# Seven half-depth products for the branch and last projections of a hybrid mLSTM and attention block

## The chip, the cores and the metric

The kernel is one program on one core of a Trainium2 chip. The metric is the device time of one execution in microseconds (us), here the median of several runs on the same chip. Engines are called as the profile calls them: PE is TensorE's matrix products, PEld its loads of the stationary operand, DVE is VectorE, ACT is ScalarE, POOL is GpSimd, and SP is the queue that issues most DMAs. A line such as L291 is a line of the kernel before.

## The reference

One layer on x of 1024 x 1024 in float32: a norm, one wide projection by w_in, an mLSTM branch in two directions, a branch of differential attention, and then the part that the change concerns, the tail:

```python
y_a = hm * jax.nn.sigmoid(a_o) * jax.nn.silu(a_z)
...
y_b = att.reshape(B, S, DA_WIDTH).astype(x.dtype) * jax.nn.silu(b_z)
gb = gate_b[layer]
mix = (jax.nn.sigmoid(g_a + gb[0]) * jnp.einsum('bsc,cd->bsd', y_a, w_branch_a[layer])
       + jax.nn.sigmoid(g_b + gb[1]) * jnp.einsum('bsc,cd->bsd', y_b, w_branch_b[layer]))
x = x + jnp.einsum('bsd,de->bse', mix, w_out[layer])
return rmsnorm(x, final_g)
```

Each of the three products is 1024 x 1024 by 1024 x 1024.

## The kernel before

Every operand of a float32 product is split into a high half H (the value rounded to the type that TensorE multiplies) and a low half L (what the rounding left), and a product is the three terms H·H, H·L and L·H. So an output block of 128 x 512 over a depth of 1024, which is 8 blocks of 128, takes 24 matmuls. A split is a copy on ACT for H and a subtraction on VectorE or POOL for L.

The program is a list of units, most of them a few matmuls with what follows them, in an order written out by hand in `build` (from L1463 on) and partly interleaved by `Weaver`. `run` goes through the list. TensorE keeps the order of the list. The instructions of the other engines and of SP are put in order by a scheduler that takes what is ready, earlier units first; on the chip each engine then goes through its own list in order. A tile of a pool has a tag and a number of buffers; a new tile of the tag waits until the instructions that use the old one are done.

**The stage that has seven products already.** The projections of the mLSTM branch (L1472 to L1542) take their output columns in 16 pairs of blocks of 128. A pair with both halves of the sequence (512 columns of the moving operand each) is four output blocks of 128 x 512, that is a 2 x 2 product of 2 x 2 blocks with a depth of 512 each. `pair_units` (L270) makes it in seven products (f = 0 to 6) of sums and differences of the blocks, 12 matmuls each, in place of eight. `load_form` (L230) makes the stationary form of product f: forms 0, 4 and 6 are blocks as they are, 1, 2, 3 and 5 are sums, made by POOL (L243, L254); then ACT rounds H (L262) and VectorE (f = 0, 4, 6) or POOL makes L (L264). A form takes half a weight slot; `run` loads forms up to four keys past the next one, six half slots in all. The moving forms (`hH`, `hL`, `TH`, `TL`) are made once in the opening. Products 0, 1, 2 and 6 add up in one PSUM bank X, with ACT copies of it taken after 0, 1 and 2 (L298); 3 and 5 in a bank G, 4 in a bank F. A sink gets the finished blocks. In the order of the list (L1538), product 0 of a pair is followed by 6 of the pair before, 3, 5 of the pair before, 1, 4, 2.

**The tail.** After the mLSTM part the last three of sixteen gate projections run (`gate_units`, three groups of 48 matmuls), the last of them woven with loads of yb by `load_y` (L1310): a DMA of 128 x 1024 into one of two raw buffers, a copy on ACT (L1314), a subtraction on VectorE (L1315). Then `mix_units` for branch b and for branch a: for each of 8 blocks of output columns and each half of the sequence, 24 matmuls through `proj` (L429); the weights of the next block come through one DMA, one ACT copy (L204) and one POOL subtraction (L209). Its `done` multiplies by the gate (L1339), or adds the second branch to the mix and splits it (L1341 to L1345). The operands ya and the rows of w_out (`load_wo`, L1369 and L1370) are loaded and split in the course of the passes. `out_units` makes the last projection in 8 blocks of rows x 2 halves, 24 matmuls each (L1399); the last half of the last block is cut in two of 256 columns. Then come the residual (L1403), the sum of squares on ACT (L1405), the norm (`rsqrt`, with its power on POOL, L147), and the stores (L1418, L1420).

Of the kernel before, what the change touches and what calls it, by code (L numbers as in the profile page):

```python
# [109 lines left out]
class Block:  # L110
    def __init__(self, tc, A):
        self.tc, self.nc, self.A = tc, tc.nc, A
        nc = self.nc
        self.v, self.a, self.p, self.t, self.q = nc.vector, nc.scalar, nc.gpsimd, nc.tensor, nc.sync
        self.wt = {}
        self.raws = {}
        self.ml, self.opening, self.ahead, self.terms, self.forms = False, True, False, {}, 0
        self.rs, self.tk, self.loaded = {}, {}, set()
# [58 lines left out]
    def load_w(self, key, nxt=None):  # L177
# [3 lines left out]
        if key[0] == "sw":  # L181
            return self.load_form(key)
# [29 lines left out]
        if nxt and self.ahead:  # L212
            self.load_raw(("w_in", OFF["bq"] + nxt[1] * 128) if nxt[0] == "rope" else nxt)
# [5 lines left out]
    def pair_raws(self, p):  # L219
        if p >= len(self.pairs) or p in self.praws:  # L220
            return
        self.praws[p] = raws = []
        for seg, i in self.pairs[p]:
            pool = self.wpool if p % 2 == 0 else self.s0
            t = pool.tile([128, 8, 128], F32, name="raw", tag="raw", **({} if p % 2 == 0 else dict(bufs=2)))
            o = OFF[seg] + 128 * i
            self.q.dma_start(out=t, in_=self.A["w_in"][0][:, o:o + 128].rearrange("(k p) e -> p k e", p=128))
            raws.append(t)

    def load_form(self, key):  # L230
        _, p, f = key
        a, g = self.a, self.p
        self.pair_raws(p)
        if p == 0:
            self.pair_raws(1)
        r1, r2 = self.praws[p]
# [4 lines left out]
        lo, hi = slice(0, 4), slice(4, 8)  # L241
        tmp = lambda n: self.s0.tile([128, 4, 128], F32, name=n, tag=n, bufs=1)
        sub = lambda out, x, y: g.tensor_tensor(out=out, in0=x, in1=y, op=ALU.subtract)  # L243
        if f == 0:
            src = r1[:, lo]
        elif f == 1:
            self.s2f = src = tmp("s2f")
            sub(src, self.s1f, r1[:, lo])
        elif f == 2:
            src = tmp("s3f")  # L250
            sub(src, r1[:, lo], r2[:, lo])
        elif f == 3:
            self.s1f = src = tmp("s1f")
            g.tensor_tensor(out=src, in0=r2[:, lo], in1=r2[:, hi], op=ALU.add)  # L254
        elif f == 4:
            src = r1[:, hi]
        elif f == 5:
            src = self.s2f
            sub(src, r1[:, hi], src)
        else:  # L260
            src = r2[:, hi]
# [4 lines left out]
        if f == 5:  # L266
            del self.praws[p]
            self.pair_raws(p + 2)

    def pair_units(self, p, sink):  # L270
# [3 lines left out]
        v, a = self.v, self.a  # L274
        B = lambda half, o: (self.hH[half][:, o:o + 4], self.hL[half][:, o:o + 4])
        T = lambda i: (self.TH[i], self.TL[i])

        plan = lambda: (B(0, 0), T(1), T(2), T(0), B(0, 4), B(1, 4), T(3))
        box = {}
        u = lambda n, bufs=1: self.s0.tile([128, 512], F32, name=n, tag=n, bufs=bufs)  # L280

        def product(f, k0):
            bH, bL = plan()[f]
# [4 lines left out]
            wH, wL = self.wt[("sw", p, f)]  # L288
# [19 lines left out]
        return [[Unit(6 * MM, lambda f=f, k0=k0: product(f, k0), (("sw", p, f),)) for k0 in (0, 2)] for f in range(7)]  # L308
# [77 lines left out]
    def run(self, units):  # L386
# [10 lines left out]
        for i, u in enumerate(units):  # L397
            if u.keys:
                need = max(order.index(k) for k in u.keys) + 1

                room = lambda k: sum(1 if x[0] == "sw" else 2 for x in self.wt) + (1 if k[0] == "sw" else 2) <= 6
                ahead = lambda k: nxt < need or nxt <= need + (4 if k[0] == "sw" else 1) and room(k)
                while nxt < len(order) and (order[nxt] in self.loaded or not self.opening
                                            and (order[nxt][0] != "sw" or hasattr(self, "_s0")) and ahead(order[nxt])):
# [905 lines left out]
    def load_y(self, src, i, slot):  # L1310
        raw = self.wy.tile([128, S], F32, name="yraw", tag="yraw", bufs=2)
        self.q.dma_start(out=raw, in_=src[i])
        h, l = slot("H"), slot("L")
        self.a.copy(h, raw)  # L1314
        self.v.tensor_tensor(out=l, in0=raw, in1=h.bitcast(F32), op=ALU.subtract)  # L1315
        return h, l

    def slot(self, which, dt=F32R):
        pool, bufs = {"yb": (self.wy, 16), "mb": (self.wy, 8), "r": (self.wr, 16)}[which]
        return pool.tile([128, S], dt, name="sl_" + which, tag=which, bufs=bufs)  # L1320

    def mix_units(self, seg, st):
        v, a, p, q = self.v, self.a, self.p, self.q

        def start(i):
            t = self.wy.tile([128, S], F32, name="tgl", tag="tgl", bufs=2)
            q.dma_start(out=t, in_=self.tg[seg][i])
            st["tg"] = t
            if seg == "gb":
                st["m", i] = self.slot("mb", F32)  # L1330
            else:
                w = "r" if i < 4 else "mb" if i < 7 else "yb"
                st["mix", i] = (self.slot(w), self.slot(w))

        def done(i, half, ps):
            c = slice(half * 512, (half + 1) * 512)
            t, m = st["tg"][:, c], st["m", i][:, c]
            if seg == "gb":
                v.scalar_tensor_tensor(out=m, in0=t, scalar=1.0, in1=ps, op0=ALU.add, op1=ALU.mult)  # L1339
                return  # L1340
            v.scalar_tensor_tensor(out=t, in0=t, scalar=1.0, in1=ps, op0=ALU.add, op1=ALU.mult)  # L1341
            v.tensor_tensor(out=m, in0=m, in1=t, op=ALU.add)
            H, Lo = st["mix", i]
            a.mul(H[:, c], m, 0.5)
            v.scalar_tensor_tensor(out=Lo[:, c], in0=m, scalar=0.5, in1=H[:, c].bitcast(F32), op0=ALU.mult, op1=ALU.subtract)  # L1345

        w = "w_branch_b" if seg == "gb" else "w_branch_a"
        un = []
        for i in range(8):
            un.append(Unit(0.0, lambda i=i: start(i)))  # L1350
            for half in range(2):
                c = slice(half * 512, (half + 1) * 512)
                un += self.proj((w, 128 * i), half, lambda ps, i=i, half=half: done(i, half, ps),
                                lambda k, c=c: (st[seg, k][0][:, c], st[seg, k][1][:, c]))
        return un

    def load_wo(self, k, st, which):
        row = self.A["w_out"][0][k * 128:(k + 1) * 128, :]
        flat = lambda t: t.rearrange("p k e -> p (k e)")
        if which == "w":  # L1360
            raw, h, l = (flat(self.wpool.tile([128, 8, 128], dt, name=f"wo{n}", tag=n))
                         for n, dt in (("raw", F32), ("wH", F32R), ("wL", F32R)))
        else:
            raw = self.wy.tile([128, D], F32, name="yraw", tag="yraw", bufs=2)
            h, l = self.slot(which), self.slot(which)
        self.q.dma_start(out=raw, in_=row)
        st["wo", k] = (h, l)
        for c in (slice(0, 512), slice(512, 1024)):
# [272 lines left out]
```

## Time and profile before

| what | us |
|---|---|
| median of 3 runs (1685.4 to 1689.81) | 1687.04 |
| span of the profiled execution | 1685.6 |
| PE busy in it | 1645.8 |
| DVE, ACT, POOL busy | 992.4, 760.3, 635.2 |
| granted TensorE clock, share of full | 0.999 |

A profile is of one execution. Its span runs from the first to the last instruction; it stands 1.4 us under the median of the runs. A busy engine is one that has an instruction under way; for PE the ends of matmuls are modelled, so the pace of matmuls is taken from the distance of their starts. In a row of the timeline stand the start, the duration, engine, line, operation, output and inputs, shapes, a count, and in brackets how long the engine had been idle and what ended it.

### The profile page before, as it was taken

What the parts mean: (1) busy time and instruction counts of PE and PEld (TensorE: products, weight loads), DVE (VectorE), ACT (ScalarE), POOL (GpSimd) and SP (SyncE); (2) the same over time, 40 slices, a digit from 0 to 9 for tenths busy, and PEclk for the clock granted to TensorE, in tenths of its full rate; (3) what the DMA queues carried; (4) which work ended last, traced back from release to release, by engine and by line L of the source; (5) the groups of instructions that cost most, each with busy time, mean ns of one, the idle gap of its engine ahead of it and who ended that gap; (6) DMA issues with size and microseconds to landing.
All of it is one profiled execution on the core that took longest, in us unless ns stands there. A gap on an engine that the chain in (4) does not pass through costs nothing. (4 is left out here: it accounts for less than half of the span.)

```text
span 1685.6 us, 25370 instructions
## 1 busy us (share of the span) xinstructions
PE 1645.8 (98%) x9431; PEld 1385.3 (82%) x9431; DVE 992.4 (59%) x1799; ACT 760.3 (45%) x1522; POOL 635.2 (38%) x712
## 2 busy tenths in 40 slices
PE   7999999999999999999999999999999999999998
PEld 5777887887877988898888888899999877888887
DVE  5778678675286766666666665325666754135533
ACT  7454555553255454444445445334655644122221
POOL 5767676655343334333451332122322412212000
PEclk9999999999999999999999999999999999999999
DMA  5334434434231213211322222166455337344222
GB/s 180 101 117 137 138 113 137 126 125 127 74 80 48 74 38 88 51 51 39 100 59 56 62 58 70 57 181 176 144 160 161 89 117 244 126 149 126 88 93 83
DMA packets 175630, 178.79 MB, mean 106 GB/s; under 512 B 12185, under 2 KB 135410, under 8 KB 175506
## 3 DMA queue, kind: packets, MB, share of 16 engines
q1 hardware_dynamic: 174594, 175.58, 34.8%
q8 instruction: 74, 1.21, 0.3%
q10 hardware_dynamic: 912, 1.59, 0.2%
q14 instruction: 50, 0.41, 0.1%
HBM read 114.11 MB, written 46.24 MB: 95 GB/s over the span
## 5 line engine op out<-in xcount | busy, mean ns | idle before, releaser
L429 PE MATMUL pj<-hH,wH 128*128 128x512 f32 x640 | 265.8, 415 | 3.3 <-ACT f L542 1.5
L429 PE MATMUL pj<-hH,wL 128*128 128x512 f32 x640 | 251.3, 393 | 1.8 <-POOL wL L207 1.8
L429 PE MATMUL pj<-hL,wH 128*128 128x512 f32 x640 | 250.1, 391 | 0.2 <-DVE hL L580 0.2
L209 POOL TENSOR_TENSOR wL<-raw,wH 128x1024 fp32r<-128x1024 f32 x41 | 99.7, 2432 | 278.0 <-ACT wH L204 268.3
L928 ACT ACTIVATE e<-S,nm 128x1024 f32<-128x1024 f32 x128 | 142.7, 1115 | 134.1 <-DVE nm L926 133.9
L948 DVE TENSOR_TENSOR pL<-T,pH 128x512 fp32r<-128x512 f32 x128 | 87.9, 688 | 117.4 <-ACT pH L947 116.7
L926 DVE TENSOR_REDUCE nm<-S 128x1 f32<-128x1024 f32 x128 | 150.5, 1217 | 10.1 <-PE S L923 9.3
L451 PE MATMUL pj<-wH,hH 128*128 128x256 f32 x512 | 149.9, 293 | 1.6 <-DVE vL L1035 1.4
L429 PEld LDWEIGHTS pj<-hH,wH 128*128 128x128 f32 x640 | 120.4, 188 | 37.7 <-issue 14.1
L451 PE MATMUL pj<-wL,hH 128*128 128x256 f32 x512 | 144.9, 283 | 1.4 <-POOL wL L207 1.4
L429 PEld LDWEIGHTS pj<-hH,wL 128*128 128x128 f32 x640 | 120.1, 188 | 30.2 <-POOL wL L207 3.4
L451 PE MATMUL pj<-wH,hL 128*128 128x256 f32 x512 | 144.5, 282 | 0.0
L429 PEld LDWEIGHTS pj<-hL,wH 128*128 128x128 f32 x640 | 120.7, 189 | 18.2 <-DVE hL L580 0.6
L429 PE MATMUL pj<-sl_yb,wH 128*128 128x512 f32 x384 | 118.9, 390 | 2.1 <-DVE sl_mb L1339 1.6
L947 ACT CAST pH<-T 128x512 fp32r<-128x512 f32 x128 | 74.7, 584 | 100.5 <-PE T L131 99.8
L204 ACT CAST wH<-raw 128x1024 fp32r<-128x1024 f32 x56 | 58.8, 1050 | 114.7 <-PE pj L429 75.8
L923 PE MATMUL S<-kst,qq 64*128 64x512 f32 x768 | 106.5, 408 | 0.0
L451 PEld LDWEIGHTS pj<-wH,hH 128*128 128x128 f32 x512 | 97.7, 191 | 6.8 <-issue 3.9
L451 PEld LDWEIGHTS pj<-wL,hH 128*128 128x128 f32 x512 | 97.5, 190 | 2.3 <-POOL wL L207 2.3
L451 PEld LDWEIGHTS pj<-wH,hL 128*128 128x128 f32 x512 | 97.7, 191 | 0.1
L934 DVE SCALAR_TENSOR_TENSOR e<-e,r,e 128x1024 f32<-128x1024 f32 x64 | 88.9, 1389 | 2.2
L923 PEld LDWEIGHTS S<-kst,qq 64*128 64x128 f32 x768 | 67.8, 184 | 26.2 <-issue 10.5
(358 smaller groups left out, 4101.4 us busy)
## 6 DMA issues: line engine op xcount, KB each, us to landing
raw<-in_w_in_dram SPq DMA_DIRECT2D x88, 512.0 KB, 3.9
kst<-hl SPq DMA_DIRECT2D x64, 128.0 KB, 2.4
qq<-hl SPq DMA_DIRECT2D x64, 128.0 KB, 2.4
x<-in_x_dram SPq DMA_DIRECT2D x8, 512.0 KB, 6.2
cak<-y SPq DMA_DIRECT2D x16, 256.0 KB, 2.3
cakH<-cin SPq DMA_DIRECT2D x16, 256.0 KB, 4.4
cakL<-tz SPq DMA_DIRECT2D x16, 256.0 KB, 4.1
gm<-oz SPq DMA_DIRECT2D x16, 256.0 KB, 2.8
```

The costliest lines, as they stand in the source:

```text
L204: self.a.copy(wH, raw)
L209: self.p.tensor_tensor(out=wL, in0=raw, in1=wHf, op=ALU.subtract)
L429: self.t.matmul(ps, lhsT=l[:, k, :], rhs=r, start=(n == 0), stop=(n == 23))
L451: self.t.matmul(ps[:, i, :], lhsT=l, rhs=r[:, k, :], start=(kh == 0 and k == 0 and m == 0), stop=(kh == 1 and k == 3 and m == 2))
L923: self.t.matmul(ps[:, o], lhsT=qq[r, x, c], rhs=k[r, y, o], start=(m == 0), stop=(m == 2))
L926: v.tensor_reduce(out=nm, in_=ps, axis=AX.X, op=ALU.max, negate=True)
L928: a.activation(out=e, in_=ps, func=AF.Exp, bias=nm[:, 0:1], accum_out=Z[:, j, t:t + 1])
L934: v.scalar_tensor_tensor(out=e0, in0=e, scalar=r[:, 0:1], in1=e0, op0=ALU.mult, op1=ALU.add)
L947: a.copy(pH[:, :, s], ps)
L948: v.tensor_tensor(out=pL[:, :, s], in0=ps, in1=pH[:, :, s].bitcast(F32), op=ALU.subtract)
```

## The change

The three products of the tail are made in the seven-product form too, each as four pairs, twelve pairs in all: four of branch b ("tw" 0 to 3), four of branch a ("tw" 4 to 7), four of the last projection ("mx" 0 to 3). They are called pairs 0 to 11. In a branch a pair is two blocks of 128 columns of w_branch, stationary, against ya or yb, moving. In the last projection it is two blocks of 128 positions of the mix, stationary, against w_out, moving; the mix stays in one tile M in float32.

The moving operand of each projection is now made on the spot by `tail_forms`: four quarters Q11, Q12, Q21 and Q22 (each 4 blocks of 128 x 512, four DMAs of 256 KB), and from them seven forms H0 to H6 with L0 to L6. The sums overwrite Q11 three times and Q12 once. Everything lives in 17 places F0 to F16 of 128 x 4 x 512: nine from the start of the tail, eight more when the memory of the normalised input falls free after the last gate product. A form's place is given to the next projection's form as soon as the last product that reads it is issued. So the forms of branch a are made while pairs 3 and 4 run, those of w_out while pairs 7 and 8 run; those of branch b partly before the last gate product, the rest after it.

```diff
+    def tail_forms(self, load, first=False):
+        v, a, p = self.v, self.a, self.p
...
+        def minus(out, x, y, eng):
+            for k in range(4):
+                eng.tensor_tensor(out=F[out][:, k], in0=F[x][:, k], in1=F[y][:, k], op=ALU.subtract)
+
+        def high(i, x):
+            take(f"H{i}")
+            for k in range(4):
+                a.copy(F[f"H{i}"][:, k], F[x][:, k])
+
+        def low(i, x):
+            take(f"L{i}")
+            for k in range(4):
+                v.tensor_tensor(out=F[f"L{i}"][:, k], in0=F[x][:, k], in1=f32(f"H{i}")[:, k], op=ALU.subtract)
+
+        t1, t2 = f(minus, "Q11", "Q12", "Q11", v), f(minus, "Q11", "Q22", "Q11", v)
+        t3, t4 = f(minus, "Q12", "Q22", "Q12", p), f(minus, "Q11", "Q21", "Q11", p)
...
+        mid = [l(1, "Q11"), t4, h(4, "Q21"), l(4, "Q21"), d("Q21"), h(2, "Q12"), l(2, "Q12"), d("Q12")]
+        last = [(h(6, "Q11"), l(6, "Q11"), d("Q11"), h(5, "Q22")), (l(5, "Q22"), d("Q22"))]
+        if first:
+            steps = [(g("Q11"),), (g("Q12"),), (g("Q22"),), (h(0, "Q11"),), (g("Q21"),), (l(0, "Q11"),), (t1,), (h(3, "Q11"), t3),
+                     (l(3, "Q11"),), (t2,), (h(1, "Q11"),)], [mid[:2], mid[2:5], mid[5:]] + last
+        else:
+            steps = [(g("Q11"), g("Q12"), g("Q22")), (h(0, "Q11"), l(0, "Q11"), t1, t3), (h(3, "Q11"), l(3, "Q11"), t2),
+                     (g("Q21"), h(1, "Q11")), mid[:3], mid[3:]] + last
```

`load_form` takes a kind; for the weights it uses three raw buffers (two "raw", one "raw2") in place of four, and for "mx" the blocks of M. `run` lets forms be made ahead as before, but those of "mx" only from a unit `ready` on, which stands behind product 6 of pair 7; the very first one is made by `early_form` during pair 7. The sinks follow.

```diff
+    def mix_sink(self, seg, n):
...
+            if rest is not None:
+                to = rest if i == j == 1 else ps
+                v.tensor_tensor(out=to, in0=ps, in1=rest, op=ALU.add)
+                ps = to
             if seg == "gb":
                 v.scalar_tensor_tensor(out=m, in0=t, scalar=1.0, in1=ps, op0=ALU.add, op1=ALU.mult)
+            else:
+                v.scalar_tensor_tensor(out=t, in0=t, scalar=1.0, in1=ps, op0=ALU.add, op1=ALU.mult)
+                v.tensor_tensor(out=m, in0=m, in1=t, op=ALU.add)
...
+            for i, (x, g) in enumerate(chain):
...
+                w.add(*s[0])
+                if i == 8:
+                    w.add(*x[0][:1], *y[6], ready, *eo[6], *o[6], do(gain), *x[0][1:], *y[5], *eo[5], *o[7], *x[3])
+                else:
+                    w.add(*x[0], *e[0], *s[1], *y[6], *eo[6], *o[6], *x[3], *e[3], *s[2], *y[5], *eo[5], *o[7])
+                w.add(*(g if i else []), *x[1], *e[1], *s[3], *x[4], *e[4], *s[4], *([early_form] if i == 7 else []),
+                      *x[2], *e[2], *s[5])
+            w.add(*x[5], *x[6])
```

Here x is the pair at hand, y the pair before, s and o the steps that make the next projection's forms, e and eo the units that give places back, g the loads of the two gate blocks (or, in the last projection, of the residual). `out_sink` does what `out_units` did, for blocks of 128 x 512 throughout: add, scale by 0.5 and add the residual, sum of squares, and with the second half of a row block the norm and the two stores. PSUM has six banks T in the tail, where the tail before used two banks pj. `load_y`, `slot`, `mix_units`, `load_wo` and `out_units` go.

More of the change, by code (lines that the diff above doesn't have):

```diff
@@ L1307, in ml_units @@
         return un, prev["O"](0) + prev["g"](1) + prev["scale"](4) + prev["scale"](6) + prev["O"](1)
[L1310 to L1320, printed above, removed]
@@ L1347, in mix_units @@
[L1347 to L1368, printed above, removed]
-            self.a.copy(h[:, c], raw[:, c])
-            self.v.tensor_tensor(out=l[:, c], in0=raw[:, c], in1=h[:, c].bitcast(F32), op=ALU.subtract)
@@ L1534, in build @@
                     more.setdefault((i + (k + step * j) // 14, (k + step * j) % 14), []).append(u)
-            products = [self.pair_units(i, sinks[i]) for i in range(len(self.pairs))]
+            products = [self.pair_units("sw", i, sinks[i], self.plan_h) for i in range(len(sw))]
             for i, x in enumerate(products + [None]):
```

289 lines of the change are left out of this document (153 added, 136 removed).

## The prediction

> **What bounds the kernel now.** The page comes first: which engine is full, and where in the span.
>
> ```profile
> PE 1645.8 (98%) x9431; PEld 1385.3 (82%) x9431; DVE 992.4 (59%) x1799; ACT 760.3 (45%) x1522; POOL 635.2 (38%) x712
> PE   7999999999999999999999999999999999999998
> ```
>
> TensorE is busy from end to end, so a matmul less is time less, as long as nothing new makes TensorE wait. Next the chain of work that ended last, with the two stretches that the change replaces, and the timeline of TensorE at their ends:
>
> ```profile
> 1508.67 82.36 PE pj L429 x362
> 1591.02 76.17 PE pj L1399 x336
> ...
> 1413.49 0.61 PE L429 MATMUL pj<-sl_yb,wH 128*128 128x512 f32 x2
> 1672.46 1.24 PE L1399 MATMUL pj<-sl_yb,sl_r 128*128 128x256 f32 x9
> 1677.85 0.52 PE L1399 MATMUL pj<-sl_r,sl_yb 128*128 128x256 f32 x3
> ```
>
> The tail (both branch projections, then the last) runs on TensorE from 1413.49 to 1678.37, 264.9 us. Its pace is 76.17 / 336 = 0.2267 us a matmul of 512 columns. It holds 2 x 384 of these in the branches and 360 in the last projection, 1128 x 0.2267 = 255.7 us, and 48 of 256 columns from 1672.46 to 1678.37, 5.9 us. That leaves 3.3 us of waits. The windows show what the other engines do meanwhile:
>
> ```profile
> core 0: us, PE busy (x) PEld busy (x) DVE busy (x) ACT busy (x) POOL busy (x), PEclk, DMA share, GB/s
> 67.00:398.00 331.00, 326.15 (x1409) 257.88 (x1409) 242.18 (x369) 175.22 (x316) 221.37 (x197) 1.00 0.41 127
> 1388.00:1413.50 25.50, 25.50 (x115) 21.10 (x114) 8.76 (x6) 10.65 (x12) 4.85 (x2) 1.00 0.87 280
> 1413.50:1591.00 177.50, 175.38 (x770) 143.97 (x769) 70.86 (x85) 42.71 (x54) 34.96 (x14) 1.00 0.42 132
> 1591.00:1678.40 87.40, 87.37 (x409) 73.14 (x407) 32.25 (x87) 18.10 (x42) 3.80 (x7) 1.00 0.25 92
> ```
>
> In the tail (last two rows) VectorE is busy 39% and POOL 15%; there is room. The first row is the older stage that already multiplies with seven half-depth products (L291): VectorE 73%, POOL 67%, and TensorE full but for little, as L291's own answer shows:
>
> ```profile
> its engine sat idle before it (us, times) until:
>   ACT u L298: 8.4, 9
>   POOL wL L264: 1.7, 2
>   DVE pj L326: 1.7, 2
>   DVE cin L355: 1.2, 2
>   ACT wL L262: 0.3, 1
> ```
>
> 13.3 us for 16 pairs, 0.83 us a pair. But there the moving operands are made once and serve all 16 pairs; in the tail each set serves four.
>
> **What the change removes.** Twelve pairs x 7 products x 12 matmuls are 1008, 228.5 us. That is 261.6 - 228.5 = **33.1 us less** of matmuls, and the 3.3 us of waits go with the old order: 36.4 us to be had.
>
> **What it adds: loads.** Operands stay at 12 MB, in 48 DMAs of 256 KB for 24 of 512 KB; the weights' 16 column blocks stay.
>
> ```profile
> raw<-in_w_branch_b_dram SPq DMA_DIRECT2D x8, 512.0 KB, 4.9
> yraw<-yb SPq DMA_DIRECT2D x8, 512.0 KB, 4.1
> ```
>
> I cost them at nothing: three quarters of the next operand are loaded a projection's length early, and a block of weights needs 4.9 us where forms are made five products, 13.6 us, ahead. With that cover gone, by SP's in-order queue standing at a gate load that waits for a late sink, it is 4.9 us a pair.
>
> **Forms.** Prices:
>
> ```profile
> L264 DVE TENSOR_TENSOR wL<-raw,wL x23: 672/684/1834, 70.7 to 358.4; 128x512 fp32r<-128x512 f32 x23
> L264 POOL TENSOR_TENSOR wL<-s1f,wL x9: 1283/1292/1749, 70.3 to 363.7; 128x512 fp32r<-128x512 f32 x9
> L262 ACT CAST wL<-raw x23: 617/622/661, 70.1 to 355.8; 128x512 fp32r<-128x512 f32 x23
> L298 ACT COPY u<-T x32: 567/586/596, 78.0 to 390.7; 128x512 f32<-128x512 f32 x32
> ```
>
> Weight forms, per pair: 7 ACT copies, 3 low halves on VectorE, 4 sums and 4 low halves on POOL (8 x 1.29 = 10.3 us). With 3 copies out of PSUM, ACT has 6.1 us. Operand forms, per projection: 28 ACT copies (17.4 us), 28 low halves and 8 sums on VectorE, 8 sums on POOL. A pair takes 84 x 0.2267 = 19.0 us, so each engine alone has time. But the maxima above (1834 against a median of 684, 1749 against 1292) say that VectorE and POOL stop each other:
>
> ```profile
> 318.05 1.81 DVE L264 TENSOR_TENSOR wL<-raw,wL 128x512 fp32r<-128x512 f32 x1
> ...
> 318.02 1.29 POOL L264 TENSOR_TENSOR wH<-s3f,wH 128x512 fp32r<-128x512 f32 x1
> 319.39 1.62 POOL L243 TENSOR_TENSOR s3f<-raw 128x512 f32<-128x512 f32 x1
> ...
> 1431.26 1.34 DVE L1339 SCALAR_TENSOR_TENSOR sl_mb<-tgl,pj 128x512 f32<-128x512 f32 x2
> 1431.11 2.48 POOL L209 TENSOR_TENSOR wL<-raw,wH 128x1024 fp32r<-128x1024 f32 x1 [10.84 <-ACT wH L204]
> ```
>
> POOL's operation ends at 319.31; VectorE's, begun 0.03 after it, ends at 319.86: it waited, then took 0.55. POOL's next ends at 321.01. So one of each costs 1.70 us when both have work, and they take turns: 0.55 for VectorE's (**D**), 1.15 for POOL's (**P**). The last two rows show the exception: with one input in PSUM, two VectorE operations take 0.67 each beside POOL. All low halves and sums of the change are D or P.
>
> A plain pair is 8 P + 4 D (one sink adds two SBUF blocks), 11.4 us, and 4 D more where the second branch adds into the mix: 13.6 of 19.0. It fits. Making one operand set is 36 D + 8 P = 29.0 us, and it can't be spread: the first place falls free after the first product of the old projection's last pair, Q11 and Q12 are overwritten in turn, and the last form is due at product 5 of the next pair. So it is counted in windows, a product being 12 x 0.2267 = 2.72 us; products run in the order 0, 6 of the pair before, 3, 5 of the pair before, 1, 4, 2.
>
> - **Branch b to branch a** (pairs 3, 4, 5). From the end of pair 3's first product to the start of pair 4's product 5, 16 products, 43.5 us. Weight forms: 17 products less 5 made ahead are 12, with 14 P + 5 D; sinks have 4 D. In all 45 D + 22 P = 24.8 + 25.3 = 50.1 us, 6.6 over at best. VectorE also does 12 operations on PSUM at 0.69, 8.3 us in the same queue: if none hides under a P, 14.9 over. I take 9.5. (ACT has 17.4 + 2.3 x 6.1 = 31 us: within.)
> - **Branch a to the last projection** (7, 8, 9). The same with 10 D of sinks: 51 D + 22 P = 53.4 us, 9.9 over, 18.2 at most. Besides, the first sum of mixed blocks waits for the mix of pair 7's product 6, with one and a half products, 4.1 us, to go: 2 x 0.69 on VectorE, then 1.29 + 0.62 + 1.29 make 4.6, 0.5 late if VectorE is free. I take 13 in all.
> - **Start** (pair 0). Operands come in beside the last gate products, where the DMA rings are 87% busy already; the first can be there at about 1394, two loads after the first yb:
>
> ```profile
> 1392.04 1.05 ACT L1314 CAST sl_yb<-yraw 128x1024 fp32r<-128x1024 f32 x1 [4.82 <-DMA yraw<-yb]
> ```
>
>   Product 5 of pair 0 starts 8 products after 1413.5, at 1435.3, 41.3 us on. 41 D + 18 P and two gate splits like that of 1431.11, 5.0 us, are 48.2, 6.9 over. If the weight forms come before the operands it is nothing; if no operation on PSUM hides, 11. I take 4.
> - **Plain pairs**: the other eight, between nothing and 0.83 us each. I take 3 in all.
> - **End**: the last block is 512 columns wide, no longer cut, with the block before it finishing in the same queues:
>
> ```profile
> 1661.78 0.69 DVE L1403 TENSOR_TENSOR xr<-pj,xr 128x512 f32<-128x512 f32 x1 [1.56 <-PE pj L1399]
> 1662.55 0.63 ACT L1405 ACTIVATE sqo<-xr 128x512 f32<-128x512 f32 x1 [2.36 <-DVE xr L1403]
> 1678.41 0.42 DVE L1403 TENSOR_TENSOR xr<-pj,xr 128x256 f32<-128x256 f32 x1 [1.47 <-PE pj L1399]
> 1678.93 0.42 ACT L1405 ACTIVATE sqo<-xr 128x256 f32<-128x256 f32 x1 [2.37 <-DVE xr L1403]
> ```
>
>   0.69 for 0.42 and 0.63 for 0.42, and up to 0.5 of queue: 1 us.
>
> The new waits are VectorE's low halves: behind them in its queue stand sinks and the weights' low halves, and TensorE waits for these. **Sum**: 1685.6 - 36.4 + 9.5 + 13 + 4 + 3 + 1 = 1679.7 us of span. The profiled span stands 1.4 below the median of the runs (1687.04), so the time is **1681 us**, 0.4% faster.
>
> **Rivals.**
>
> 1. *The operands hide as in the older stage.* For it: 0.83 us a pair there, with POOL at 67%. Against: no set is made under way there. Waits are 12 x 0.83 and 2 at the start, 12 us: 1687.0 - 36.4 + 12 + 1 = **1664 us**. Chance 0.20.
> 2. *Slower: VectorE's queue sets the handovers.* Its instructions go in order; each stands for the whole POOL operation before it, at full lengths 0.69 and 1.29. Price: 45 x 0.69 + 22 x 1.29 = 59.4, 15.9 over; with 51 D 63.6, 20.1 over, and 2 for the mix's sink behind low halves that aren't due yet; start 41 x 0.69 + 18 x 1.29 + 5.0 = 56.5, 15.2 over. With 4 for plain pairs and 1 at the end: 1687.0 - 36.4 + 58 = **1709 us**. It is slower once waits pass 35.4 us. For it: the 1.81 us row, and sinks that stand in the same queue. Against: that row's overlap of 0.14, and the L1339 row. Chance 0.28. The Trainium skill, page "SBUF — State Buffer", section "Who interferes with whom", has this as a rule: a VectorE instruction with two SBUF inputs and a GpSimd one that reads SBUF exclude each other for the whole instruction, and the second fully blocks. The rows agree on the blocking; one of each costs 1.70 us in them, not the 1.98 of whole lengths.
>
> **How the numbers follow.** My case, 1668 to 1695 us, has 0.52. Runs of this kernel tell about 0.3%, 5 us, from no change: 1682 to 1692. Of my case 0.28 lies below 1682, 0.22 within, 0.02 above; of rival 2, 0.02 falls within. Faster 0.20 + 0.28 = 0.48, same 0.24, slower 0.28. The range runs from 1660, rival 1 with its plain pairs nearly free of waits, to 1702, which leaves out the worse part of rival 2.
>
> **What would show it.** After, 1008 matmuls should stand in the tail at 0.2267 us. TensorE's idle time by releaser should name VectorE's low halves, some 9 us in pairs 3 to 5 and 13 in 7 to 9, in pieces under 2 us, and VectorE's mean for them be near 1 us, not 0.69. If it names POOL's sums or ACT's copies, the price of a form is wrong; if DMA, the loads aren't hidden. If the waits in the tail are under 15 us, D and P pass each other more than these rows show; over 35, the queue has it.

## The result and the profile after

The changed kernel takes 1734.51 us (median of 4 runs, 1731.37 to 1735.46) against 1686.99 us for the kernel before on the same chip: a ratio of 1.0276, 95% interval 1.0264 to 1.0288. It is 47.5 us slower. The profiled execution has a span of 1732.2 us, 46.6 more than before. Lines of the kernel are from here on those of the changed kernel: product matmuls L298, copies of the unfinished sum X L305, casts of weight forms L269, their low halves L271 and sums L250 and L261; of the operands' forms the sums are L1347, the casts L1352, the low halves L1357.

The page of the changed kernel first, busy time and the slices:

```profile
PE 1640.2 (95%) x9263; PEld 1372.1 (79%) x9263; DVE 1115.0 (64%) x1922; ACT 820.3 (47%) x1660; POOL 776.2 (45%) x816
PE   7999999999999999999999999999999989889687
...
PEclk9999999999999999999999999999999999989898
```

168 matmuls are gone, as they should be, but PE's busy time fell by only 5.6 us of the 33.1 that they were worth, and six of its last eight slices are no longer full. The third row is new, too: the mean granted clock is under nine tenths in three of these eight. One window over the tail, from the first product matmul to the last:

```profile
core 0: us, PE busy (x) PEld busy (x) DVE busy (x) ACT busy (x) POOL busy (x), PEclk, DMA share, GB/s
1418.26:1723.39 305.13, 254.39 (x1009) 201.09 (x1007) 211.67 (x274) 118.78 (x226) 168.38 (x117) 0.91 0.30 100
```

The tail starts 4.8 us later (1418.26 against 1413.49), lasts 305.1 us against 264.9, and the rest after it is 1.6 us longer: 46.6 in all. Of the 305.1, PE is idle for 50.7 us and busy for 254.4, where 1008 matmuls at 0.2267 us would be 228.5. What PE waited for, by releaser, from 1390 to the end:

```profile
PE T L298 <- ACT u L305: 36.1, 12, 8.9
PE T L298 <- ACT p L305: 7.1, 1, 7.1
PE T L298 <- ACT wL L269: 5.8, 1, 5.8
PE pj L442 <- ACT gt L850: 2.7, 1, 2.7
PE T L298 <- DVE u L1421: 1.5, 1, 1.5
PE T L298 <- POOL wL L271: 0.3, 1, 0.3
```

The columns are the sum, the number of waits and the longest. No row names VectorE's low halves; ACT's copies of X have 43.2 of the 53.5 us. The timeline shows what stands ahead of such a copy, with PE, ACT, VectorE and POOL around two of the handovers' waits:

```profile
1508.63 4.36 PE L298 MATMUL T<-F,wL 128*128 128x512 f32 x12 [7.85 <-ACT u L305]
1611.76 5.49 PE L298 MATMUL T<-F,wL 128*128 128x512 f32 x12 [8.87 <-ACT u L305]
...
1505.03 2.37 ACT L1352 CAST F<-F 128x512 fp32r<-128x512 f32 x4 [4.69 <-DVE F L1347]
1507.30 0.61 ACT L269 CAST wL<-s1f 128x512 fp32r<-128x512 f32 x1
1507.99 0.58 ACT L305 COPY u<-T 128x512 f32<-128x512 f32 x1
...
1597.09 4.68 DVE L1347 TENSOR_TENSOR F<-F,F 128x512 f32<-128x512 f32 x4
...
1597.84 6.75 POOL L1347 TENSOR_TENSOR F<-F,F 128x512 f32<-128x512 f32 x4 [1.23 <-DVE F L1347]
```

The matmuls before the first wait were over at 1500.8. The copy came at 1507.99, since ACT's queue stood at a cast that waited 4.69 us for VectorE's sums. These four sums themselves took only 2.48 us (from 1504.26 on, with POOL idle); they were late because of what stood ahead of them in VectorE's queue. The last two rows, of the second handover, show such work: four sums on each engine at the same time take POOL 1.69 us apiece and VectorE 1.17. So it is over the whole tail; groups of VectorE, then of POOL (busy us, mean ns):

```profile
L1357 DVE TENSOR_TENSOR F<-F,F 128x512 fp32r<-128x512 f32 x72 | 67.4, 987 | 5.9 <-ACT F L1352 5.9
L1347 DVE TENSOR_TENSOR F<-F,F 128x512 f32<-128x512 f32 x16 | 15.4, 1022 | 0.0
...
L1347 POOL TENSOR_TENSOR F<-F,F 128x512 f32<-128x512 f32 x20 | 35.5, 1800 | 10.3 <-DVE F L1357 8.4 <-DVE F L1347 1.9
```

Last the clock, in windows that begin with the first matmul after a wait (PE busy, clock, DMA):

```profile
1445.76:1449.76 4.00, 4.00 (x17) 1.00 0.08 14
1568.09:1572.09 4.00, 4.00 (x17) 1.00 0.07 11
1650.90:1654.90 4.00, 4.00 (x11) 0.57 0.01 2
1697.77:1701.77 4.00, 4.00 (x12) 0.68 0.01 2
1508.63:1511.63 3.00, 3.00 (x7) 0.52 0.97 296
1518.97:1524.97 6.00, 6.00 (x14) 0.50 0.00 0
```

The waits ahead of them were 0.9, 1.2, 2.1, 2.3, 7.9 and 3.2 us. After the first two the clock stays full; after each of the others it is at a half for some microseconds. Windows over the half-clock stretches behind all nine waits of more than 2 us in the tail hold 39.4 us of PE's busy time at a clock of 0.50, so 19.7 us of it is lost time. The prediction had every matmul at 0.2267 us.

The waits of the pairs that make no operand set look alike but have another source. Around the wait of 0.89 us that ended at 1445.76:

```profile
1444.61 0.62 ACT L269 CAST wL<-s1f 128x512 fp32r<-128x512 f32 x1 [3.37 <-POOL s1f L250]
1445.13 0.58 ACT L305 COPY u<-T 128x512 f32<-128x512 f32 x1
...
1443.29 1.29 POOL L250 TENSOR_TENSOR s1f<-s1f,raw 128x512 f32<-128x512 f32 x1
```

The copy stands behind the cast of a weight form that isn't due yet, and the cast waits for GpSimd's sum. The sum takes 1.29 us, its time without any hindrance: this wait is made by GpSimd's own pace. Ahead of all eight such waits of the plain pairs (0.8 to 1.3 us in the branches, 2.1 to 2.3 in the last projection, 11.8 us in all) ACT has a cast that stood 2.45 to 3.83 us for GpSimd's sum; that sum takes 1.28 or 1.29 us in six of the eight and 1.59 in two.

### The profile page after: what moved, and what is told of

It reads as the page before. It is cut to its first block, busy times and chain, and to the rows that moved or that the text cites. A ratio compares the mean times of both kernels' runs of the same rounds, so it can differ in the third digit from the quotient of the medians.

```text
span 1732.2 us, 25508 instructions
## 1 busy us (share of the span) xinstructions
PE 1640.2 (95%) x9263; PEld 1372.1 (79%) x9263; DVE 1115.0 (64%) x1922; ACT 820.3 (47%) x1660; POOL 776.2 (45%) x816
## 3 DMA queue, kind: packets, MB, share of 16 engines
q10 hardware_dynamic: 912, 1.59, 0.2%
## 5 line engine op out<-in xcount | busy, mean ns | idle before, releaser
L298 PE MATMUL T<-F,wL 128*128 128x512 f32 x504 | 134.6, 419 | 30.4 <-ACT u L305 24.3
L442 PEld LDWEIGHTS pj<-hH,wH 128*128 128x128 f32 x640 | 121.3, 189 | 40.4 <-issue 15.2
L298 PE MATMUL T<-F,wH 128*128 128x512 f32 x504 | 131.0, 411 | 20.3 <-ACT u L305 11.7
L298 PEld LDWEIGHTS T<-F,wL 128*128 128x128 f32 x504 | 101.4, 203 | 57.2 <-ACT u L305 26.9
L442 PEld LDWEIGHTS pj<-hH,wL 128*128 128x128 f32 x640 | 121.0, 189 | 29.7 <-POOL wL L207 2.6
L298 PEld LDWEIGHTS T<-F,wH 128*128 128x128 f32 x504 | 99.8, 200 | 46.5 <-ACT u L305 14.4
L209 POOL TENSOR_TENSOR wL<-raw,wH 128x1024 fp32r<-128x1024 f32 x25 | 59.9, 2397 | 137.5 <-ACT wH L204 135.1
```

Of the source, the lines that this page charges most:

```text
L209: self.p.tensor_tensor(out=wL, in0=raw, in1=wHf, op=ALU.subtract)
L298: self.t.matmul(ps, lhsT=l[:, k, :], rhs=r[:, k, :], start=(first and k == 0 and m == 0), stop=(k == 3 and m == 2), skip_group_check=not f ...
L442: self.t.matmul(ps, lhsT=l[:, k, :], rhs=r, start=(n == 0), stop=(n == 23))
```

## The experiments

Theory 1: VectorE and POOL shut each other out while operand forms are made, and what comes late from them ends up as PE's waits. Rival A: ACT's order does it, a copy behind casts that aren't due. Rival B: VectorE simply has too much to do, whatever POOL does. A third possibility is that what GpSimd makes simply comes late, because it takes 1.29 us where VectorE takes 0.68. Beside these stands the question whether waits slow down the matmuls behind them. All ratios are to the kernel before on the same chip.

**Everything on VectorE.** GpSimd makes nothing in the tail.

```diff
-        a, g = self.a, self.p
+        a, g = self.a, self.p if kind == "sw" else self.v
...
-        t3, t4 = f(minus, "Q12", "Q22", "Q12", p), f(minus, "Q11", "Q21", "Q11", p)
+        t3, t4 = f(minus, "Q12", "Q22", "Q12", v), f(minus, "Q11", "Q21", "Q11", v)
```

> Same work; all sums and low halves of the last 300 us that GpSimd made (t3, t4, the sums of the weights' forms and their low halves) are VectorE's, and GpSimd is idle there. Theory 1: a VectorE sum takes 0.62 us again instead of 0.98 to 1.04, two on VectorE 1.2 us against 1.70 us for one on each; 67 such and the sinks fill about 50 us per window of 43.5 us: each handover is late by 4 to 9 us instead of 15 to 17, 1695 to 1712 us with fewer slow matmuls. The rival of VectorE's load alone: 22 more instructions of 0.6 us per set, each handover later by 13 us: 1755 to 1770 us. The rival of ScalarE's order: no less than 1725 us, since the copies still stand behind casts that wait for sums.

Measured: 1696.45 us, ratio 1.0049 (1.0030 to 1.0069). VectorE got twice as many sums of operands, and those of the weights, and the kernel became 38 us faster. Its groups:

```profile
L1357 DVE TENSOR_TENSOR F<-F,F 128x512 fp32r<-128x512 f32 x70 | 44.1, 684 | 0.2 <-ACT F L1352 0.2
L1347 DVE TENSOR_TENSOR F<-F,F 128x512 f32<-128x512 f32 x32 | 19.8, 683 | 0.0
```

987 and 1022 ns became 684 and 683. Rivals A and B, which had it at 1725 and 1755 us or more, fall as main causes. But the 38 us are not all the exclusion's. PE's waits fell from 53.5 to 28.2 us, and of these 25.3 us the plain pairs' waits are 11.8 (none is left), the two handovers' 9.9, the gate wait 2.7 and the start's 0.9; the rest of the 38 us is mostly half clock that went with them. The plain pairs' part goes with the pace of GpSimd's sums. How the handovers' part divides between exclusion and pace isn't shown by this run.

**POOL works for nobody.** To the last kernel come subtractions on GpSimd, into a tile that nothing reads.

```diff
...
+        if kind != "sw" and f in (1, 2, 3, 5) and hasattr(self, "noise"):
+            for _ in range(2):
+                self.p.tensor_tensor(out=self.noise.rearrange("p (k e) -> p k e", k=4), in0=H.bitcast(F32),
+                                     in1=self.noise.rearrange("p (k e) -> p k e", k=4), op=ALU.subtract)
...
                 a.copy(F[f"H{i}"][:, k], F[x][:, k])
+                if i in (3, 4) and hasattr(self, "noise"):
+                    p.tensor_tensor(out=self.noise, in0=f32(f"H{i}")[:, k], in1=self.noise, op=ALU.subtract)
...
```

> The run with all sums on VectorE, and beside them on GpSimd subtractions of 128x512 that nothing waits for: as many, and at about the same places, as GpSimd has in the changed kernel (two for each of four forms of a pair, eight for each set of operands after the first). Theory 1 (exclusion): VectorE's low halves and sums go from 0.62 us back to about 1.0 us in the handovers, and the time goes up from 1696 to 1715 to 1740 us although no instruction waits for GpSimd. The rival that GpSimd cost time because others waited for its results: VectorE keeps 0.62 us and the time stays at 1694 to 1699 us.

Measured: 1768.15 us, ratio 1.0474 (1.0443 to 1.0504), 72 us more than without the subtractions. VectorE's groups in it:

```profile
L1362 DVE TENSOR_TENSOR F<-F,F 128x512 fp32r<-128x512 f32 x71 | 66.8, 992 | 0.0
L1350 DVE TENSOR_TENSOR F<-F,F 128x512 f32<-128x512 f32 x32 | 32.7, 1084 | 0.0
```

These are the same two groups (the added lines move their numbers), at 992 and 1084 ns again. No wait of ACT's in the tail names GpSimd here, and VectorE waits for it only 4.0 us, for a small operation of the norm at the end that every kernel here has. So work beside VectorE costs by itself, without anything being late from GpSimd: the exclusion is shown. The run doesn't show that lateness costs nothing in the changed kernel. Between the start and the first handover PE has no wait at all here, so the subtractions don't bring back the plain pairs' short waits there. The time went 28 us beyond the 1740 expected; that VectorE has all the sums here and is held up as well would explain it, but wasn't tried.

**Waits and the clock, by themselves.** In the kernel before, PE waits at five places of the branch projections for a chain of ACT copies.

```diff
...
+                    for _ in range(self.gaps.get(self.count, 0)):
+                        self.a.copy(self.old, self.old)
+                    if self.count in self.gaps:
+                        self.a.copy(self.zz, self.old[:, 0:32])
+                        self.t.matmul(box["ps"][0:32, 0:32], lhsT=self.zz, rhs=self.zz, start=True, stop=True)
...
```

> The kernel before, with waits put into its branch projections: at five places, 33 us or more apart, TensorE waits for a chain of 2, 4, 8, 16 and 6 copies on ScalarE, of about 0.5 us each, and one small matmul follows each chain. Clock theory: after the waits of 4 us and more the next 12 to 24 matmuls run at up to twice 0.227 us, 1.5 to 3 us lost at each, nothing after 1 us; 5 to 10 us in all beyond the waits. Rival (the slow matmuls of the changed kernel come from its transfers or its operands): every matmul after the waits takes 0.227 us and the time grows by the waits alone, about 20 us.

Measured: 1739.69 us, ratio 1.0306 (1.0276 to 1.0336); the span grew by 51.1 us. The waits answer for its tail, and windows from the first matmul after each of the five waits:

```profile
PE pj L430 <- ACT zz L429: 30.6, 5, 10.8
```

```profile
1437.65:1443.65 6.00, 6.00 (x15) 0.52 0.80 263
1476.91:1481.91 5.00, 5.00 (x16) 0.66 0.47 151
1517.61:1522.61 5.00, 5.00 (x14) 0.56 0.22 65
1564.80:1570.80 6.00, 6.00 (x17) 0.59 0.00 0
1610.54:1614.54 4.00, 4.00 (x11) 0.57 0.00 0
```

The waits were 7.30, 2.86, 5.26, 10.78 and 4.44 us long. Behind every one the clock is at a half for 3 to 6 us, with busy DMA or none, and with the operands of the kernel before. Window length times missing clock gives 2.9, 1.7, 2.2, 2.5 and 1.7 us, 11.0 in all: about 2.2 us for each wait, whether it was 3 or 11 us long. None of the waits came out short, so the expectation's "nothing after 1 us" isn't tried here. The remainder of the 51.1 us, after 29.1 us by which the waits grew (the kernel before has 1.5 us more of others), has two more parts: the scheduler put 22 gate matmuls (39 after 1410 us against 17) ahead of the tail, 5 us, and the matmuls between the waits are a little slow at full clock (the last section), about 6 us.

**ACT in written order.** A copy then stands right behind its product, ahead of casts written after it.

```diff
...
             w.weave([do(places)] + early, rest[cut:])
+            w.add(keep(E.PE, E.Activation))
```

> Same work; ScalarE's instructions are kept in written order from the start of the last 300 us, in which a copy of an unfinished sum stands right behind its product and ahead of the casts written after it (and the form of product 5 is written ahead of that of product 3, without which this order can't run). The rival of ScalarE's order: the waits of the plain pairs (0.8 to 1.2 us, 2.3 us twice) go and the handovers' 32 us shrink to half or less, with the slow matmuls: 1690 to 1705 us. Theory 1 and the rival of VectorE's load: the copy comes earlier, but TensorE then waits for the sums and casts themselves: the handovers keep at least 28 of their 32 us, 1722 to 1734 us.

Measured: 1724.19 us, ratio 1.0214 (1.0175 to 1.0253). The waits for u copies fell from 36.1 to 29.7 us; 9.0, 3.2 and 2.6 us were left in the first handover, 7.1, 2.9 and 4.8 in the second. The plain pairs' waits in the branches are gone. Rival A is worth 10 us, not the main cause.

**No low halves of operands.** The plan gives H for L, too, which leaves the term with the operands' low halves without its values.

```diff
...
-            for k in range(4):
-                v.tensor_tensor(out=F[f"L{i}"][:, k], in0=F[x][:, k], in1=f32(f"H{i}")[:, k], op=ALU.subtract)
...
-        plan = lambda i: (F[f"H{i}"], F[f"L{i}"])
+        plan = lambda i: (F[f"H{i}"], F[f"H{i}"])
```

> The changed kernel without the low halves of the operands' forms: each product multiplies with the high half three times, 28 VectorE instructions fewer per set; GpSimd's work and all casts stay. Theory 1: 17 to 23 VectorE instructions beside 22 of GpSimd take about 40 us of the 43.5 us window, so the handovers' waits go to 6 us or less each, and with them two thirds of the slow matmuls: 1695 to 1708 us. The rival of ScalarE's order: the casts of summed weights still wait for GpSimd and the copies still stand behind them: at least half of the waits stay, 1712 to 1725 us.

Measured: 1709.72 us, ratio 1.0128 (1.0098 to 1.0157), between the two expectations. The first handover's waits went from 15.4 to 8.0 us (4.9, 1.8 and 1.3), the second's from 14.7 to 6.9 (6.3 and 0.6), more than theory 1 had; the 6.4 us at the start and 0.8 to 3.8 us in the other pairs stayed. So VectorE's work in the handovers is half of what is late there; it doesn't tell exclusion from load, which the first two runs do.

**No second and third set**, in the changed kernel:

```diff
-            planA, endA, prepA = self.tail_forms(part(self.ya))
+            planA, endA, prepA = planB, {}, []
```

(and the same for w_out).

> Leaves out the second and third set of operand forms: all twelve pairs multiply with the forms of yb, so no operand is loaded, subtracted, cast or halved after the first set. The weights' forms, the copies of the unfinished sums and the sinks stay. Theory 1 (VectorE and GpSimd shut each other out while the sets are made) and the rival of VectorE's load alone both expect the two handovers' waits (15.4 and 16.8 us) to go, with most of the 26 us of slow matmuls behind them: 1682 to 1692 us. The rival of ScalarE's order (a copy stands behind casts that wait) expects the 7.2 us at the start and the waits of 0.8 to 2.3 us of the plain pairs to stay, about 1.0 us on every pair. If the slow matmuls are not made by the waits, only 32 us go and it stays at 1700 to 1704 us.

Measured: 1695.33 us, ratio 1.0043 (1.0023 to 1.0063), 39 us less, and in none of the ranges expected. The handovers' waits are gone, but the start's wait is 13.1 us here and the other pairs keep waits of 0.3 to 3.8 us, which is why it isn't quicker. The bound run further down, which differs from it by GpSimd's work and by the place of the first set's steps, is 37 us quicker still, and has none of these waits but one: the plain pairs' waits are there as long as GpSimd makes the sums of the weights' forms, even without a second and third set.

**Steps of the first set between the products of pair 0**, everything on VectorE:

```diff
-            w.add(leave("h"), enter("wr", "wr"), do(lambda: self.spare.extend(range(self.RIGHT, 17))), *left)
+            w.add(leave("h"), enter("wr", "wr"), do(lambda: self.spare.extend(range(self.RIGHT, 17))), *left[:1])
...
+                if i == 0:
+                    w.add(*x[0], left[1], *x[3], left[2])
...
```

> The run with all sums on VectorE, and the last four of the six remaining steps of the first set stand between the first products of pair 0 instead of ahead of them. The 6.3 us at the start, where the first copy stands behind 16 casts, fall to 2 us or less, with the half pace behind them (2 to 2.5 us): 1688 to 1692 us. If the copy is held by the sums and not by the casts ahead of it, the start stays: 1695 to 1698 us.

Measured: 1688.66 us, ratio 1.0003 (0.9991 to 1.0014). The wait at the start is gone: before, the first copy stood behind sixteen casts, at 1424.66 in the run with everything on VectorE, and here it stands behind three, at 1419.11. So the start's wait was made by the order in ACT's queue. 21.7 us of waits are left in the tail, and that is the point at which the change neither wins nor loses.

The same with ACT in written order:

> The same as the run before it, with ScalarE kept in written order from the start of the last 300 us (form 5 written ahead of form 3). If what is left in the handovers is ScalarE's order, the 11.8 us of waits for copies go, with half of the slow matmuls: 1674 to 1682 us. If it is VectorE's 50 us of sums per window of 43.5 us, the wait only moves from the copies to the casts: within 3 us of the run before it.

Measured: 1691.85 us, ratio 1.0018 (1.0007 to 1.0029). Waits moved from the handovers (2.6, 2.8 and 0.6 us in the first, for 5.6 and 2.9) to a new one of 3.3 us early in the tail, at 1434 us. ACT's order isn't what is left.

**The same without second and third set**, the bound for everything that can be done about the handovers:

> The run with all sums on VectorE and the first set's steps between the products of pair 0, without the second and third set of operand forms: pairs 4 to 11 multiply with the forms of yb. Theory 1: without VectorE's sums of the handovers and without GpSimd nothing holds TensorE but short ends; of 1688.7 us go the 19 us of waits and the 8 to 11 us of slow matmuls behind them: 1657 to 1664 us, which is the time that the prediction gave to a change whose waits are hidden. If the slow matmuls were not made by waits, 1668 to 1673 us.

Measured: 1658.66 us, ratio 0.9824 (0.9801 to 0.9848). The window over its tail:

```profile
1413.98:1647.93 233.95, 232.50 (x1009) 188.93 (x1007) 168.58 (x294) 89.98 (x169) 3.46 (x7) 1.00 0.29 94
```

One wait of 1.46 us is left, the clock is 1.00, and the same 1008 matmuls keep PE busy for 232.5 us instead of 254.4. So 21.9 us of the changed kernel's matmul time go with its waits, and the half clock counted above is 19.7 of them. Beside the waits this run lacks the making of the forms of ya and w_out, so the rest of the 21.9 needn't be the waits'.

**Steps cut up and dealt out** evenly among the half products, four or so instructions at a time; in one kernel with VectorE and ACT in written order, in the other with the scheduler's:

```diff
+            def mix(small, big):
+                out, n, m = [], len(small), len(big)
+                for j, u in enumerate(big):
+                    out += [u] + small[j * n // m:(j + 1) * n // m]
+                return out
...
+                    w.add(*x[0], *e[0], *mix(s[1], y[6] + x[3]), *e[3], *mix(s[2], y[5] + g + x[1]), *e[1], *mix(s[3], x[4]), *e[4],
...
```

> The same work as the run with the first set's steps between the products of pair 0; the steps of the second and third set are cut into single instructions and dealt out evenly among the half products, and VectorE and ScalarE keep the written order from pair 1 on, so that a sink or a copy never stands behind more than four to six instructions of a set. If the queues' order is what is left, the waits of 21 us fall to 8 us or less and the slow matmuls by two thirds: 1667 to 1676 us. If VectorE's load (about 50 us in 43.5 us) is what is left, the waits move to casts and low halves and keep 12 to 16 us: 1680 to 1690 us.

> The same cutting and dealing out, with VectorE's and ScalarE's order left to the scheduler, which puts what is ready first. If the written order is what helps, this stays within 4 us of the 1688.7 us of the uncut steps; if the dealing out itself helps, it comes out within 3 us of the run with the written order.

Measured: 1739.96 us in written order, ratio 1.0306 (1.0283 to 1.0330), and 1682.67 us in the scheduler's, 0.9971 (0.9958 to 0.9985). The first missed both expectations by 50 us: PE waits 42 us for u copies, in pairs without a set as well. ACT's queue in pair 2, and a row of VectorE's:

```profile
1472.71 0.62 ACT L269 CAST wH<-s1f 128x512 fp32r<-128x512 f32 x1 [5.30 <-DVE s1f L261]
1476.10 0.62 ACT L269 CAST wL<-s1f 128x512 fp32r<-128x512 f32 x1 [2.77 <-DVE s1f L250]
1476.62 0.58 ACT L305 COPY u<-T 128x512 f32<-128x512 f32 x1
...
1471.93 0.69 DVE L261 TENSOR_TENSOR s1f<-raw 128x512 f32<-128x512 f32 x1 [4.28 <-DMA raw<-in_w_branch_b_dram]
```

The written order has casts of forms that are due later ahead of the copies, and VectorE, in order too, stood 4.28 us at a block of weights that was still on its way. The second did better than the uncut steps by 6 us, so the dealing out helps and the written order hurts; its waits in order of time:

```profile
1508.96 4.76 PE L298 MATMUL T<-F,wH 128*128 128x512 f32 x12 [5.43 <-ACT u L305]
...
1576.05 3.03 PE L298 MATMUL T<-F,wL 128*128 128x512 f32 x12 [1.67 <-ACT u L305]
...
1582.48 3.04 PE L298 MATMUL T<-F,wH 128*128 128x512 f32 x12 [2.01 <-DVE u L1388]
1593.08 5.31 PE L298 MATMUL T<-F,wL 128*128 128x512 f32 x12 [7.55 <-ACT wL L269]
```

**Forms 5 and 6 later**, and products 6 and 5 of pair 7 ahead of the second half of product 0 of pair 8:

```diff
-                    w.add(*x[0][:1], *mix(o[5], y[6]), ready, *eo[6], *mix(o[6], [do(gain)] + x[0][1:] + y[5]), *eo[5], *mix(o[7], x[3] + g + x[1]))
+                    w.add(*x[0][:1], *mix(o[5], y[6]), ready, *eo[6], do(gain), *y[5], *x[0][1:], *eo[5], *mix(o[6], x[3]), *mix(o[7], g + x[1]))
```

(and o[6], o[7] one to two products later in pair 4).

> The run with dealt-out steps and the scheduler's own order (1682.67 us), with the forms of products 5 and 6 of the second and third set made one to two products later, and with products 6 and 5 of pair 7 done ahead of the second half of product 0 of pair 8. In that run TensorE waits 7.55 us for the first summed weight form of pair 8, and VectorE makes the low halves of products 5 and 6 ahead of the sum that this form waits for. If that is the cause, the wait falls to 2 to 4 us and the 5.43 us in pair 4 to 3 us or less, with 2 us of slow matmuls: 1672 to 1678 us. If VectorE's total load sets it, the same microseconds come back at the next product: 1680 to 1685 us.

Measured: 1679.75 us, ratio 0.9949 (0.9935 to 0.9963), between the two expectations. The waits answer of its tail:

```profile
PE T L298 <- ACT u L305: 4.6, 2, 3.2
PE T L298 <- ACT wL L269: 4.1, 1, 4.1
PE T L298 <- DVE u L1388: 3.8, 2, 3.4
```

The 7.55 us became 4.1 and the 5.43 became 3.2, but 3.4 us instead of 2.0 stand at the product ahead: part of it came back, as VectorE's load has it. This version computes all that the changed one does; it takes 3.2% less than that one and 0.5% less than the kernel before.

## Why the prediction was wrong

The sum was 1679.7 us of span; the span is 1732.2. The 52.5 us between them come apart like this:

| step | predicted | measured |
|---|---|---|
| handover b to a (pairs 3, 4, 5) | 9.5 | 15.4 |
| handover a to last (pairs 7, 8, 9) | 13 | 14.7 |
| start, pair 0 | 4 | 7.2 |
| other waits of the tail | 3 | 13.4 |
| matmuls slower because of waits | 0 | 21.9 |
| pace of 1008 matmuls without waits | 228.5 | 232.5 |
| later start of the tail | 0 | 4.8 |
| end | 1 | 1.6 |

**Right:** the number of matmuls; that VectorE's and POOL's operations on SBUF exclude each other, at about 1.70 us for one of each (POOL's four at 1.69 each in the timeline), with means near 1 us; and that the sets and not the weights' forms make the long waits. The first two runs show the exclusion apart from load, and the second shows it apart from waiting. One of the prediction's own signs came true as well: over 35 us of waits, "the queue has it". The other misled: ACT's copies are named, but the price of a form held. The Trainium skill, page "SBUF — State Buffer", section "Who interferes with whom", says that the second fully blocks; that agrees with 987 ns against 684. Its hold over the whole instruction would make 1.98 us of one of each, and the rows have 1.70.

**The first step that failed: "a pace of 0.2267 us a matmul" held whatever PE waits for.** A wait was priced as a wait. The clock run shows that a wait of some microseconds costs some 2 us of matmuls on top. In the changed kernel the granted clock of 0.50 accounts for 19.7 us, and against the bound run the matmuls took 21.9 us more. With it the point from which the change loses was wrong as well: not 35.4 us of waits, as rival 2 had it, but about 22, where the run with the first set's steps between products stands at a ratio of 1.0003. The waits were also forecast in pieces under 2 us; nine in the tail were longer, up to 8.9. The Trainium skill has this on the page "TensorE: Matmul & The Clock Gate", section "Part 1: The HAM clock gate": after an idle window of about 3.4 us the array runs at half its clock until it has been busy for about as long. The half agrees, 0.50 in the windows; waits of 2.1 us were enough here, and one of 1.91 in the dealt-out run in written order (the last section).

**The second: the sizes taken between the bounds.** 9.5, 13 and 4 were put where some of VectorE's operations on PSUM hide under POOL's. The first handover measured 15.4 against the bound of 14.9 with none hidden, the second 14.7 between its bounds of 9.9 and 18.2, the start 7.2 between nothing and 11. (The 14.7 leave out 2.1 us ahead of product 6 of pair 8, which the expectations count in; its source is that of the plain pairs.) Whether hiding decided these sizes isn't shown, since each of the waits came through ACT's queue, and at the start ACT's order made it. Rival 2 came near with its sum, 58 us of waits and end against 50.7 + 4.8 + 1.6 = 57.1 measured, but by luck: it had 22.1 for the second handover, 15.2 for the start and 4 for the plain pairs, and the errors cancel. It had no slower matmuls either.

**The third: "the new waits are VectorE's low halves".** The wait comes through ACT. Product 1's copy of X has one product, 2.72 us, before product 2 needs the bank, product 2's copy has as little before product 6, and ACT's queue holds casts that wait for late sums. That is why the rows name a copy that takes 0.58 us. In the plain pairs the prediction put 3 us for short ends; 13.4 us were measured, 11.8 of them by copies behind casts that waited for GpSimd's sums, mostly at GpSimd's own pace, which is no exclusion. The prediction's own view of the older stage named this: `ACT u L298` has 8.4 of its 13.3 us. Written order of ACT alone took back 10 us, so in the handovers it is the way that lateness takes and not its source.

**Loads at nothing** held for the products: no wait of PE in the tail names a DMA. **The later start of the tail** had no term. Most of its 4.8 us are a gate wait of 2.7 us that ended at 1411.07 and the half clock behind it (PE's clock is 0.50 from 1412.5 to 1415.9). The gate's activation stood in ACT's queue behind a cast that waited 2.75 us for VectorE's sums, so this is the handovers' pattern and no load. Loads do show in a queue just after: from 1400.4 SP stood 10.5 us at a load of weights whose buffer VectorE and GpSimd still read, with the gate's stores behind it, and ACT's next gate activation waited 5.95 us for such a store (at 1418.06). What that adds to the start's 7.2 us wasn't tried.

The range, 1660 to 1702, had no price for the clock, which no step had.

## What to carry to other kernels

An elementwise operation with two SBUF inputs that was handed to GpSimd to relieve VectorE relieved nothing here, where VectorE had such operations too: giving all of them to VectorE won 38 us, in part because the two engines no longer shut each other out and in part because VectorE's sums come sooner. When a kernel that keeps TensorE full gets new waits, a wait of more than about 2 us is to be priced with about 2 us of half-speed matmuls on top. Where a short instruction is named as the releaser, look at what stands ahead of it in its engine's queue and follow that to its source before its order is changed.

## What the runs showed of the hardware that was not expected

- Subtractions on GpSimd for which nothing waits cost 72 us of the kernel's time (1768.15 against 1696.45), by holding up VectorE, whose low halves went from 684 to 992 ns.
- Near 2 to 3 us the length of a wait doesn't decide alone whether the clock falls. In the changed kernel it fell after every wait of 2.12 us and longer; in the dealt-out run it stayed full after 2.01 us (1582.48: the products behind it at 3.04 us). But in the dealt-out run in written order it fell after a wait of 1.91 us and stayed full after one of 3.04, as these windows behind the two waits show:

```profile
1453.42:1457.42 4.00, 4.00 (x11) 0.57 0.00 0
1496.00:1500.00 4.00, 4.00 (x17) 1.00 1.03 324
```

  It also stayed full after 2.28 us in the run without second and third set and after 2.72 us in the run with GpSimd's unread subtractions. What else decides wasn't tried. Once low, it stayed so for 3 to 6 us of matmuls, whatever the length of the wait.
- In the clock run, matmuls at a granted clock of 1.00 are slower than the same matmuls of the kernel before, 20 us and more after a wait:

```profile
1500.05 0.40 PE L439 MATMUL pj<-sl_yb,wL 128*128 128x512 f32 x1
...
1504.95 0.39 PE L439 MATMUL pj<-sl_yb,wL 128*128 128x512 f32 x1
```

```profile
1500.58 0.39 PE L429 MATMUL pj<-sl_yb,wL 128*128 128x512 f32 x1
...
1505.34 0.39 PE L429 MATMUL pj<-sl_r,wL 128*128 128x512 f32 x1
```

  The first fence is of the clock run, the second of the kernel before, both the timeline of PE. From the first row to the last it is 21 matmuls each time: 4.90 us, 0.233 each, against 4.76 us, 0.227. In the bound run, nearly without waits, it is 232.5 / 1008 = 0.231. What sets this pace wasn't found.
